# Max pooling over windows of 16: three shrinking load slots replaced by two shifted slots of 64 KB, and the last store issued from ScalarE

## Chip, cores and metric

One core of one Trainium2 chip. The metric is device time in microseconds (us). Before the change the median was 335.19 us in six runs (335.11 to 335.36). Lower is better.

## The reference

Each row of 4096 float32 numbers is cut into 256 windows of 16, and each window gives its maximum:

```python
x: (32, 256, 4096) float32
result[:, :, i] = np.max(x[:, :, start:end], axis=-1)   # 256 windows of 16
result: (32, 256, 256) float32
```

The input is 134.22 MB and the output 8.39 MB. There is one comparison per number read, so data movement is what can be expected to set the time. Spread over 128 partitions, each partition has 16,384 windows. "Column" below means one window of one partition: 64 B of input, 4 B of output.

## The kernel before

The kernel loads some columns of all partitions into a slot, lets VectorE reduce them to maxima, keeps the maxima in SBUF (the on-chip memory), and stores them all at the end. It has three slots, used in turn, in the same memory as the maxima. Because the maxima grow, the slots shrink: the loads have 128, 1024, 1024, then three each of 1000, 940, 884, 832 and 784, then 736 and 152 columns, 20 in all. All DMAs are issued from SyncE.

```python
    AREA = 53200
    SLOTS = 3
    MOST = 65536 // (4 * W)          # 1024 columns
    FIRST = 128
    ...
    area = pool.tile([P, AREA], fp32, tag="area", name="area")
    ...
        for i, size in enumerate(loads):
            a = b - size
            at = n_loads % SLOTS * slot_sizes[n_loads // SLOTS] * W
            slot = area[:, at : at + size * W]
            nc.sync.dma_start(out=slot, in_=xg[:, a * W : b * W])
            nc.vector.reduce_max(
                out=area[:, base + a : base + b],
                in_=slot.rearrange("p (n w) -> p n w", w=W),
                axis=mybir.AxisListType.X,
            )
    ...
    for dst, src in stores:          # three stores, after all loads
        nc.sync.dma_start(out=dst, in_=src)
```

Of the kernel before, what the change touches and what calls it, by code (L numbers as in the profile page):

```python
# [1 line left out]

# [4 lines left out]


@with_exitstack
def kernel(  # L10
    ctx: ExitStack,
    tc: tile.TileContext,
    x: bass.AP,
    output_size: bass.AP,
    out: bass.AP,
):





    nc = tc.nc
    P = nc.NUM_PARTITIONS
    fp32 = mybir.dt.float32

    B, C, L = x.shape
    O = int(output_size)
    assert L % O == 0, (L, O)
    W = L // O
    total = B * C * O // P  # L30
    assert B * C * O % P == 0

    AREA = 53200
    SLOTS = 3
    MOST = 65536 // (4 * W)
    ALIGN = 4
    FIRST = 128
    ROUNDS_A = 3
    LAST = 4


    slot_sizes = [MOST]
    rounds = [[FIRST] + [MOST] * (SLOTS - 1)]
    left = total - sum(rounds[0])
    while left:
        room = AREA - (total - left)
        n = min(room // (SLOTS * W + SLOTS) // ALIGN * ALIGN, MOST)
        if left <= slot_sizes[-1]:
            n = left
        slot_sizes.append(n)  # L50
        rounds.append([])
        while left and len(rounds[-1]) < SLOTS:
            n = min(n, left)
            rounds[-1].append(n)
            left -= n
    sizes = [n for r in rounds for n in r]
    groups = [sizes[: ROUNDS_A * SLOTS], sizes[ROUNDS_A * SLOTS :]]

    pool = ctx.enter_context(tc.tile_pool(name="pool", bufs=1))
    area = pool.tile([P, AREA], fp32, tag="area", name="area")  # L60

    xw = x.flatten_outer_dims().rearrange("r (o w) -> (r o) w", w=W)
    ow = out.flatten_outer_dims().rearrange("r o -> (r o)")

    stores = []
    n_loads = 0
    first = 0
    low = AREA
    for g, loads in enumerate(groups):
        n = sum(loads)  # L70
        xg = xw[first : first + P * n].rearrange("(p n) w -> p (n w)", p=P)
        og = ow[first : first + P * n].rearrange("(p n) -> p n", p=P)
        first += P * n
        base = low - n
        b = n
        for i, size in enumerate(loads):
            a = b - size
            at = n_loads % SLOTS * slot_sizes[n_loads // SLOTS] * W
            slot = area[:, at : at + size * W]
            nc.sync.dma_start(out=slot, in_=xg[:, a * W : b * W])  # L80
            nc.vector.reduce_max(  # L81
                out=area[:, base + a : base + b],
                in_=slot.rearrange("p (n w) -> p n w", w=W),
                axis=mybir.AxisListType.X,
            )
            n_loads += 1
            b = a
        low = base
        if g < len(groups) - 1:
            stores.append((og, area[:, base : base + n]))  # L90
        else:
            end = sum(loads[len(loads) - LAST :])
            for a, b in ((end, n), (0, end)):
                stores.append((og[:, a:b], area[:, base + a : base + b]))

    for dst, src in stores:
        nc.sync.dma_start(out=dst, in_=src)


# [1 line left out]
_INS = ['x', 'output_size']  # L101
_OUTS = [((32, 256, 256), 'float32')]

_NUMBERS = {'output_size': 256}


# [26 lines left out]
```

## Time and profile before

| | before |
|---|---|
| median time | 335.19 us |
| span of the profiled run | 333.4 us |
| VectorE busy | 276.0 us, 83% |
| packets of the DMA queue | 3312, 142.61 MB, 99.1% of 16 engines' span |
| loads and stores | 20 and 3 |

Lines of the page of the kernel before. "q1" is the queue that SyncE feeds; the last number of its line is the time that its packets took, as a share of 16 engines' span. In the line of VectorE (DVE) the figures are busy time and mean ns of one reduction, then the time that the engine stood idle and what ended it.

```profile
span 333.4 us, 112 instructions
DVE 276.0 (83%) x20; POOL 0.2 (0%) x4
q1 hardware_dynamic: 3312, 142.61, 99.1%
L81 DVE TENSOR_REDUCE area<-area 128x1000 f32<-128x16000 f32 (+8 forms) x20 | 276.0, 13806 | 49.1 <-DMA area<-in_x_dram 49.1
```

The DMA engines are full and VectorE waits for them and for nothing else. The timeline of the same run shows the rhythm: start, duration, then what ran, and in brackets the idle time before it.

```profile
63.17 16.82 DVE L81 TENSOR_REDUCE area<-area 128x1000 f32<-128x16000 f32 x1 [1.69 <-DMA area<-in_x_dram]
82.14 16.82 DVE L81 TENSOR_REDUCE area<-area 128x1000 f32<-128x16000 f32 x1 [2.15 <-DMA area<-in_x_dram]
...
294.93 30.58 SPq L97 DMA_DIRECT2D out_dram<-area  x3
296.14 13.22 DVE L81 TENSOR_REDUCE area<-area 128x784 f32<-128x12544 f32 x1 [1.62 <-DMA area<-in_x_dram]
310.14 15.01 DVE L81 TENSOR_REDUCE area<-area 128x736 f32<-128x11776 f32 x2 [0.77 <-DMA area<-in_x_dram]
```

A load of 1000 columns (8.19 MB) lands every 18.9 us, and its reduction takes 16.8. The last reduction ends at 325.15 us; the two large stores were issued long before and keep the DMA engines busy past that moment.

The trace also records every DMA packet, one for each row of a partition: 8 rows per DMA on each of the 16 engines, followed on each engine by a packet of 4 B (0.009 us), here called the semaphore packet. A row of 64,000 B took 2.361 us, one of 9,728 B 0.371 us.

### The profile page before, as it was taken

The page shows a single profiled execution, that of the slowest core. Times are in us where ns is not written, and L with a number is a line of the kernel's source. Part 1 is how long each engine was busy: PE and PEld are TensorE (multiplying, and loading weights), DVE is VectorE, ACT ScalarE, POOL GpSimd, SP SyncE. Part 2 cuts the span into 40 slices and gives each one's busy share as a digit, 9 for nine tenths or more (in the row PEclk, how much of TensorE's full clock was granted, in tenths as well). Part 3 has the DMA queues.
Part 4 walks back from the last instruction along what each step waited for, and adds up shares of the span by engine and source line. Part 5 has one row for each costly group of instructions (what it writes and reads, how often), then busy time and mean ns, then how long its engine had stood idle before and what let it go on. Part 6 is the DMA issues. An engine that isn't in the chain of part 4 may idle for free.

```text
span 333.4 us, 112 instructions
## 1 busy us (share of the span) xinstructions
DVE 276.0 (83%) x20; POOL 0.2 (0%) x4
## 2 busy tenths in 40 slices
DVE  2009979797988989797989797989898898989990
POOL 0000000000000000000000000000000000000000
DMA  9898989898999998999999999999999999989997
GB/s 377 377 503 377 503 369 491 369 491 369 491 397 433 462 462 375 433 462 441 434 434 434 434 434 415 409 441 473 415 409 470 397 470 397 470 380 452 414 431 310
DMA packets 3312, 142.61 MB, mean 428 GB/s; under 512 B 368, under 2 KB 368, under 8 KB 368
## 3 DMA queue, kind: packets, MB, share of 16 engines
q1 hardware_dynamic: 3312, 142.61, 99.1%
HBM read 134.22 MB, written 8.39 MB: 428 GB/s over the span
## 4 chain that ended last, share of the span: by engine, by line
DMA 64%; DVE 31%; DVEq 1%; another core or an unknown queue 0%; SPq 0%; issue 0%
DMA area<-in_x_dram 64%; DVE area L81 31%; DVEq L128 1%; SPq L80 0%; DVEq L81 0%
## 5 line engine op out<-in xcount | busy, mean ns | idle before, releaser
L81 DVE TENSOR_REDUCE area<-area 128x1000 f32<-128x16000 f32 (+8 forms) x20 | 276.0, 13806 | 49.1 <-DMA area<-in_x_dram 49.1
L114 POOL MEMSET const-bfloat16-1.0<- 128x1 bf16 x1 | 0.1, 102 | 0.0
L114 POOL MEMSET const-uint8-127<- 128x1 uint8 x1 | 0.1, 101 | 0.0
L114 POOL MEMSET const-float32-0.0<- 128x1 f32 x1 | 0.1, 99 | 0.2 <-issue 0.2
L114 POOL MEMSET const-float32-1.0<- 128x1 f32 x1 | 0.1, 98 | 0.0
## 6 DMA issues: line engine op xcount, KB each, us to landing
area<-in_x_dram SPq DMA_DIRECT2D x3, 8000.0 KB, 40.1
area<-in_x_dram SPq DMA_DIRECT2D x3, 7520.0 KB, 37.5
area<-in_x_dram SPq DMA_DIRECT2D x3, 7072.0 KB, 35.3
area<-in_x_dram SPq DMA_DIRECT2D x3, 6656.0 KB, 33.2
area<-in_x_dram SPq DMA_DIRECT2D x3, 6272.0 KB, 31.3
area<-in_x_dram SPq DMA_DIRECT2D x1, 5888.0 KB, 30.3
out_dram<-area SPq DMA_DIRECT2D x1, 3998.0 KB, 27.6
out_dram<-area SPq DMA_DIRECT2D x1, 2966.0 KB, 34.2
```

The costliest lines, as they stand in the source:

```text
L81: nc.vector.reduce_max(out=area[:, base + a : base + b], in_=slot.rearrange("p (n w) -> p n w", w=W), axis=mybir.AxisListType.X,)
L114: nc = _bacc.Bacc("TRN2", target_bir_lowering=False, num_devices=1)
L128: with _tile.TileContext(nc) as tc:
```

## The change

The intent: fewer and larger loads. Two slots replace three, so each can stay at 64 KB per partition (1024 columns) until the end, and 17 loads do the work of 20. With two slots a load has to wait until the one before last has been reduced. To shorten that wait, a slot is 152 columns longer than a load, and loads alternate between its low and its high end. The reduction is cut into 872 and 152 columns, in such an order that the next load overlaps only the piece that is reduced first. The first load has 132 columns. The last store (892 columns) is issued from ScalarE. The memory stays the same: 212,496 B per partition for 212,800.

```diff
-    SLOTS = 3
-    MOST = 65536 // (4 * W)
-    FIRST = 128
+    CHUNK = 1024
+    GAP = 152
+    FIRST = 132
+    LOADS_A, LOADS_B = 9, 6
     ...
+    ring = pool.tile([P, 2 * (CHUNK + GAP) * W], fp32, tag="ring", name="ring")
+    kept = pool.tile([P, total - last], fp32, tag="kept", name="kept")
     ...
+                low = n_loads % 2 * (CHUNK + GAP)
+                moved = n_loads // 2 % 2
+                at = low + moved * GAP
+                nc.sync.dma_start(out=ring[:, at * W : (at + n) * W], in_=xn)
+                if n == CHUNK:
+                    cut = CHUNK - GAP if moved else GAP
+                    parts = [(0, cut), (cut, n)]
+                    for u, v in parts if moved else parts[::-1]:
+                        pooled(dst[:, u:v], at + u, v - u)
     ...
+    nc.scalar.dma_start(out=og[:, full : full + last], in_=last_kept)
+    tc.no_sync_barrier()
     for dst, src in stores:
         nc.sync.dma_start(out=dst, in_=src)
```

(Cut: the slots of before, the grouping of the loads, and the last load, whose maxima lie in a free part of its slot.)

More of the change, by code (lines that the diff above doesn't have):

```diff
@@ L31 @@
     assert B * C * O % P == 0
-    AREA = 53200
-    SLOTS = 3
-    MOST = 65536 // (4 * W)
-    ALIGN = 4
-    FIRST = 128
-    ROUNDS_A = 3
-    LAST = 4
-    slot_sizes = [MOST]
-    rounds = [[FIRST] + [MOST] * (SLOTS - 1)]
-    left = total - sum(rounds[0])
-    while left:
-        room = AREA - (total - left)
-        n = min(room // (SLOTS * W + SLOTS) // ALIGN * ALIGN, MOST)
-        if left <= slot_sizes[-1]:
-            n = left
-        slot_sizes.append(n)
-        rounds.append([])
-        while left and len(rounds[-1]) < SLOTS:
-            n = min(n, left)
-            rounds[-1].append(n)
-            left -= n
@@ L56 @@
-    sizes = [n for r in rounds for n in r]
-    groups = [sizes[: ROUNDS_A * SLOTS], sizes[ROUNDS_A * SLOTS :]]
+    CHUNK = 1024
+    GAP = 152
+    FIRST = 132
+    LOADS_A, LOADS_B = 9, 6
+    last = total - FIRST - (LOADS_A + LOADS_B) * CHUNK
+    assert 0 < last and last * (W + 1) <= CHUNK * W
     pool = ctx.enter_context(tc.tile_pool(name="pool", bufs=1))
-    area = pool.tile([P, AREA], fp32, tag="area", name="area")
+    ring = pool.tile([P, 2 * (CHUNK + GAP) * W], fp32, tag="ring", name="ring")
@@ L62, with pooled, group @@
+    kept = pool.tile([P, total - last], fp32, tag="kept", name="kept")
     xw = x.flatten_outer_dims().rearrange("r (o w) -> (r o) w", w=W)
     ow = out.flatten_outer_dims().rearrange("r o -> (r o)")
+    def pooled(dst, at, n):
+        nc.vector.reduce_max(
+            out=dst,
+            in_=ring[:, at * W : (at + n) * W].rearrange("p (n w) -> p n w", w=W),
+            axis=mybir.AxisListType.X,
+        )
+    taken = 0
+    def group(n):
+        nonlocal taken
+        span = slice(taken * P, (taken + n) * P)
+        taken += n
+        return (
+            xw[span].rearrange("(p n) w -> p (n w)", p=P),
+            ow[span].rearrange("(p n) -> p n", p=P),
+        )
@@ L65 @@
     stores = []
     n_loads = 0
-    first = 0
-    low = AREA
-    for g, loads in enumerate(groups):
-        n = sum(loads)
-        xg = xw[first : first + P * n].rearrange("(p n) w -> p (n w)", p=P)
-        og = ow[first : first + P * n].rearrange("(p n) -> p n", p=P)
-        first += P * n
-        base = low - n
-        b = n
-        for i, size in enumerate(loads):
-            a = b - size
-            at = n_loads % SLOTS * slot_sizes[n_loads // SLOTS] * W
-            slot = area[:, at : at + size * W]
-            nc.sync.dma_start(out=slot, in_=xg[:, a * W : b * W])
-            nc.vector.reduce_max(
-                out=area[:, base + a : base + b],
-                in_=slot.rearrange("p (n w) -> p n w", w=W),
-                axis=mybir.AxisListType.X,
-            )
-            n_loads += 1
-            b = a
-        low = base
-        if g < len(groups) - 1:
-            stores.append((og, area[:, base : base + n]))
-        else:
-            end = sum(loads[len(loads) - LAST :])
-            for a, b in ((end, n), (0, end)):
-                stores.append((og[:, a:b], area[:, base + a : base + b]))
+    base = 0
@@ new lines @@
+    for g, loads in enumerate(
+        ([FIRST] + [CHUNK] * LOADS_A, [CHUNK] * LOADS_B + [last])
+    ):
+        xg, og = group(sum(loads))
+        a = 0
+        for n in loads:
+            xn = xg[:, a * W : (a + n) * W]
+            dst = kept[:, base + a : base + a + n] if n != last else None
+            if n == FIRST:
+                nc.sync.dma_start(
+                    out=ring[:, CHUNK * W : (CHUNK + n) * W], in_=xn
+                )
+                pooled(dst, CHUNK, n)
+            else:
+                low = n_loads % 2 * (CHUNK + GAP)
[7 more added lines that the diff above has]
+                        pooled(dst[:, u:v], at + u, v - u)
+                else:
+                    end = (at + CHUNK) * W
+                    last_kept = ring[:, end - n : end]
+                    pooled(last_kept, at, n)
+                n_loads += 1
+            a += n
+        full = a - last if g else a
+        stores.append((og[:, 0:full], kept[:, base : base + full]))
+        base += full
@@ L96 @@
+    assert taken == total
+    nc.scalar.dma_start(out=og[:, full : full + last], in_=last_kept)
+    tc.no_sync_barrier()
     for dst, src in stores:
```

## The prediction

> **What bounds the kernel now.** Data movement. The page's span is 333.4 us; the DMA queue's packets took 99.1% of 16 engines' span, 142.61 MB at a mean 428 GB/s, while VectorE was busy 276.0 us (83%) and its 49.1 us of idling waited on loads. In the trace's packet records a row of 64,000 B takes 2.361 us, one of 9,728 B 0.371 us; a fit over all rows gives 27.22 GB/s per engine (435.6 for 16) plus 0.0136 us per row. That agrees with the Trainium skill, "DMA: Bandwidth & Descriptors", section "Where 436 GB/s comes from" (435.2 GB/s through 16 ports). From the first packet, 1.76 us after the start, to the last end 330.3 us pass, of which packets fill 330.2 on each engine. So there is hardly a gap to win: outside lie 1.76 us at the start and 1.3 us at the end.
>
> **What the change does, costed.**
> - Bytes: unchanged; at the fitted rate 327.4 us.
> - Rows: 20 loads and 3 stores become 17 and 3, 8 rows per engine each: 184 rows per engine become 160. Saved: 24 x 0.0136 = 0.33 us, plus three semaphore packets of 0.009 us, all on the critical path.
> - VectorE: 15 loads are reduced in two pieces. Its durations fit 16.67 ns per output column plus 0.15 us, so 872 + 152 columns take 17.4 us for 17.22. Off the path: a load takes 19.35 us.
> - Two slots for three: load k+2 may go when the 872-column piece of load k is done, 14.7 us after k landed, and its packets flow about 1.1 us later (the first load: issued at 0.73, first packet at 1.76). The earliest engine runs out of load k+1 about 18.2 us after k landed (19.35 less 0.5 landing lag and 0.6 spread of the engines). About 2 us of slack, so no gap. Reducing in one piece would give 17.2 + 1.1 = 18.3 us, a tie; that is what the shifted slot buys.
> - End: after the last load lands (about 312.4 us) two stores of 7.93 MB occupy the engines for 18.4 us. The last store is issued from ScalarE 15.1 us after that landing, with packets at about 16.2, before the others drain at about 17.5. It interleaves with the second store; the Trainium skill, same page, section "Issuing engines are not separate DMA queues", says all issuers share the same 16 DMA engines, so this gains no bandwidth. Before, the last store was hidden too: issued at 325.2, its packets began at 328.5, directly behind the previous store.
> - Start: 132 columns for 128; the first packet does not move.
>
> **Prediction.** 335.2 - 0.35 = about 334.9 us, range 334.2 to 335.8. Chances: faster by over 2% 0.01, within 2% 0.97, slower by over 2% 0.02.
>
> **What would show each step.** DMA packets on the page fall from 3312 to 2880, their share staying near 99%; 65,536 B rows still take 2.42 us; reductions of 872 columns take 14.7 us and start every 19.35 us; VectorE totals about 278 us; the last reduction ends near 327.4 us, and the ScalarE store's packets lie among the second large store's.
>
> **What would make it wrong.** (1) Starvation: if issue to flow takes over 3 us in mid-stream, some 14 loads each leave a gap and landings are over 19.35 us apart. (2) The new row pitches (598,272 and 450,304 B for 511,744 and 536,832) slow HBM reads: rows take over 2.42 us. (3) The ScalarE store comes late and the engines idle at the end, or interleaving two queues is slower than one.

## The result, and the profile after

| | before | after |
|---|---|---|
| median of 6 runs each | 335.19 us | 335.05 us (334.90 to 335.14) |
| span of the profiled run | 333.4 us | 333.4 us |
| VectorE busy | 276.0 us | 276.5 us |
| DMA packets | 3312 | 2880 |

The ratio is 0.9995, with a 95% interval of 0.9983 to 1.0008. A ratio here is the mean time of one kernel's runs over that of the other's runs of the same rounds, so it is not quite the ratio of the medians. The time lies in the predicted range, and the difference is not clear of noise.

The same lines of the page after. "q10" is ScalarE's queue.

```profile
span 333.4 us, 113 instructions
DVE 276.5 (83%) x32; POOL 0.2 (0%) x4
q1 hardware_dynamic: 2736, 142.15, 98.7%
q10 hardware_dynamic: 144, 0.46, 0.3%
```

The reductions after, by shape:

```profile
L52 DVE TENSOR_REDUCE kept<-ring 128x872 f32<-128x13952 f32 x15 | 220.3, 14686 | 46.0 <-DMA ring<-in_x_dram 46.0
L52 DVE TENSOR_REDUCE kept<-ring 128x152 f32<-128x2432 f32 x15 | 40.1, 2676 | 0.0
```

The timeline after, in mid-stream and at the end:

```profile
102.58 17.28 DVE L52 TENSOR_REDUCE kept<-ring 128x872 f32<-128x13952 f32 x2 [2.07 <-DMA ring<-in_x_dram]
...
121.92 17.28 DVE L52 TENSOR_REDUCE kept<-ring 128x872 f32<-128x13952 f32 x2 [2.06 <-DMA ring<-in_x_dram]
...
313.27 15.01 DVE L52 TENSOR_REDUCE ring<-ring 128x892 f32<-128x14272 f32 x1
328.32 0.37 ACTq L109 DMA_DIRECT2D out_dram<-ring  x1
```

A load now lands every 19.35 us, 8.39 MB each time, which is 433.5 GB/s; before it was 8.19 MB in 18.9 us, 433 GB/s: the same rate. The DMA engines were full before and are full after. The chain of waits after shows how two slots work together (start, duration, what):

```profile
39.87 0.02 issue
39.88 23.97 DMA ring<-in_x_dram
63.86 0.02 issue
63.88 14.70 DVE kept L52
78.58 0.02 issue
78.59 23.96 DMA ring<-in_x_dram
```

One slot's cycle is 14.70 us until the first piece is reduced and 23.96 us from the issue of the next load to its landing: 38.7 us, two transfers of 19.35 us. Of the 23.96 us, the packet records give 3.6 us to waiting: load 3 (the small first load is load 0) was issued at 39.88 us and the earliest engine began it at 43.47. I call these 3.6 us the **lead**, the time for which a load is queued before the first engine has nothing else to do. The prediction had reckoned that about 1.1 us of it are needed and that the rest is slack. The experiments test that.

### The profile page after: what moved, and what is told of

Read it like the earlier page. It is cut to its first block, busy times and chain, and to the rows that moved or that the text cites. A ratio compares the mean times of both kernels' runs of the same rounds, so it can differ in the third digit from the quotient of the medians.

```text
span 333.4 us, 113 instructions
## 1 busy us (share of the span) xinstructions
DVE 276.5 (83%) x32; POOL 0.2 (0%) x4
## 2 busy tenths in 40 slices
DMA packets 2880, 142.61 MB, mean 428 GB/s; under 512 B 320, under 2 KB 320, under 8 KB 448
## 3 DMA queue, kind: packets, MB, share of 16 engines
q1 hardware_dynamic: 2736, 142.15, 98.7%
HBM read 134.22 MB, written 8.39 MB: 428 GB/s over the span
## 4 chain that ended last, share of the span: by engine, by line
DMA 58%; DVE 36%; DVEq 5%; issue 0%; SPq 0%
DMA ring<-in_x_dram 58%; DVE kept L52 36%; DVEq L143 5%; SPq L83 0%
## 5 line engine op out<-in xcount | busy, mean ns | idle before, releaser
L52 DVE TENSOR_REDUCE kept<-ring 128x872 f32<-128x13952 f32 (+2 forms) x31 | 261.5, 8477 | 51.8 <-DMA ring<-in_x_dram 51.8
L52 DVE TENSOR_REDUCE ring<-ring 128x892 f32<-128x14272 f32 x1 | 15.0, 15009 | 0.0
```

The lines of the kernel that those rows point to most:

```text
L52: nc.vector.reduce_max(out=dst, in_=ring[:, at * W : (at + n) * W].rearrange("p (n w) -> p n w", w=W), axis=mybir.AxisListType.X,)
```

## The experiments

Twelve kernels ran, all with correct results. The theory was that of the prediction: the time is bytes at a fixed rate plus a small cost per row, and everything else is off the path, with slack. The main rivals were that rows cost nothing, that the ScalarE store or the row pitch (the distance between rows in HBM) matters, and that the shifted slots do more than the prediction granted them.

### The changed kernel again, and its last store on SyncE

> The changed kernel once more, for comparison on the same chip. Theory (bytes at a fixed rate plus 0.0136 us per row): 334.8 to 335.2 us, 0.1 to 0.35 us under the kernel before. Rival (rows cost nothing, the 0.14 us seen is noise): the same median as the kernel before, on either side of it.

Measured: 334.95 us (334.83 to 335.00) beside 335.14 us for the kernel before, ratio 0.9993 (0.9981 to 1.0005). A second time the median is 0.1 to 0.2 us lower, which fits the theory; the interval still contains 1, so the rival is not excluded by time alone.

```diff
-    nc.scalar.dma_start(out=og[:, full : full + last], in_=last_kept)
-    tc.no_sync_barrier()
     for dst, src in stores:
         nc.sync.dma_start(out=dst, in_=src)
+    nc.sync.dma_start(out=og[:, full : full + last], in_=last_kept)
```

> The last store goes out on SyncE, behind the two large ones, as in the kernel before. Theory: the store is issued about 328.3 us, 2 us before the large stores drain, and follows them without a gap, so the time stays within 0.3 us of the changed kernel. Rival (the ScalarE store costs or gains something at the end, such as a second queue or its later flow): a difference of 0.5 to 1.5 us, in either direction.

Measured: 335.11 us, ratio to the kernel before 0.9999 (0.9987 to 1.0011). That is within 0.3 us of the changed kernel, as the theory had it. The packet records say why: the store's first packet starts at 330.32 us from ScalarE and at 330.33 us from SyncE, in both cases as the first engine finishes its large stores. Its issue, at 328.3 us, is early enough either way.

The mirror of it, the kernel before with its last store moved to ScalarE:

```diff
+    dst, src = stores.pop()
+    nc.scalar.dma_start(out=dst, in_=src)
+    tc.no_sync_barrier()
     for dst, src in stores:
         nc.sync.dma_start(out=dst, in_=src)
```

> The kernel before with only the last store (1228 KB) moved to ScalarE, ahead of the others. Theory: its bytes and rows are the same, so within 0.15 us of the kernel before. Rival (the changed kernel's 0.15 us come from the ScalarE store, since the version with that store on SyncE gave 335.11 for 334.95): 0.1 to 0.3 us faster than the kernel before.

Measured: 335.29 us beside 335.11, ratio 1.0005 (0.9992 to 1.0019). It did not get faster (0.18 us slower by the medians, a little more than the theory's 0.15), so the rival finds no support, though the interval reaches 0.3 us to the other side: the ScalarE store is worth nothing that these runs resolve. The Trainium skill, "DMA: Bandwidth & Descriptors", section "Issuing engines are not separate DMA queues", fits this: it says that all issuers end on the same 16 engines.

### What a row costs

```diff
-                nc.sync.dma_start(out=ring[:, at * W : (at + n) * W], in_=xn)
+                for u in range(0, n, PIECE):          # PIECE = 256
+                    v = min(u + PIECE, n)
+                    nc.sync.dma_start(
+                        out=ring[:, (at + u) * W : (at + v) * W],
+                        in_=xn[:, u * W : v * W],
+                    )
```

> Each load of 1024 columns goes out as four of 256: 45 or more extra loads, 8 rows per engine each. Theory (0.0136 us per row on each engine, 0.009 us per semaphore packet, all on the path): 48 extra loads, 384 extra rows per engine, 5.2 us + 0.4 us, so about 340.7 us (339.8 to 341.5), with rows of 16,384 B taking 0.615 us. Rival (rows cost nothing of their own while the queue is full): within 0.5 us of the changed kernel.

The page of this run has 6,912 more packets on SyncE's queue than that of the changed kernel (2736):

```profile
q1 hardware_dynamic: 9648, 142.15, 99.2%
```

Measured: 339.22 us (338.99 to 339.38), just under the theory's range and 4.27 us over the changed kernel of the same rounds (334.95). Rows do cost, so the rival falls; but 4.27 us over 384 rows per engine are 0.0111 us per row, semaphore packets included, where the theory had 5.6 us, or 0.0147 us per row. The rows themselves took 0.615 us each, as expected. What the sum of the records overlooked is that an engine's packets overlap a little: in this run they add up to 335.5 us per engine, while only 334.1 us pass from the first packet to the last end. With the cost measured here, the change's 24 fewer rows are worth 24 x 0.0111 = 0.27 us, an estimate from this run. The run does not part the cost of a row from that of a DMA, for here as in the change there are 8 rows per engine to a DMA.

### The slots without the shift

```diff
-                moved = n_loads // 2 % 2
+                moved = 0
...
-                    for u, v in parts if moved else parts[::-1]:
-                        pooled(dst[:, u:v], at + u, v - u)
+                    pooled(dst, at, n)
```

> No shifted slots and one reduction per load: a slot comes free 17.24 us after its load landed, for 14.7. Theory: a slot's cycle is 0.5 us landing lag + 19.35 us transfer + about 0.3 us spread + 17.24 us reduction + about 1.05 us from issue to flow = 38.45 us, and two transfers take 38.70 us, so it is a tie: within 0.5 us of the changed kernel, landings still 19.35 us apart. Rival (the shifted slot is what makes two slots work): landings 19.8 to 20.5 us apart and a time of 341 us or more.

Measured: 353.29 us (351.75 to 356.5), ratio 1.0542. The theory's "tie" was wrong by 18 us. The chain of waits of this run:

```profile
61.63 24.64 DMA ring<-in_x_dram
86.27 0.02 issue
86.30 17.23 DVE kept L52
103.53 0.02 issue
103.54 24.43 DMA ring<-in_x_dram
...
226.75 23.05 DMA ring<-in_x_dram
```

The reduction takes 17.23 us as expected. But issue to landing takes 22.5 to 24.6 us, 23.7 on average of loads 3 to 15, nearly the 23.96 us of the changed kernel, although there is now almost nothing left to wait behind. The sum of the expectation for it was 1.05 + 19.35 + 0.5 + 0.3 = 21.2 us. The packet records name the missing 2.5 us. Load 3, issued at 42.29 us, does start on the first engine at 43.47, 1.2 us later, but on the last one only at about 46.3 us. Its first rows took up to 3.1 us for the usual 2.42, and rows of later loads up to 3.8 us. From then on the 16 engines end each load up to 2.8 us apart, for 0.6 before. The slot comes free only when the slowest of them has landed, while the fastest one runs dry.

### Less shift: where does the loss begin?

```diff
+    SHIFT = 64                                  # then 16, then 112
...
-                at = low + moved * GAP
+                at = low + moved * SHIFT
...
-                    cut = CHUNK - GAP if moved else GAP
+                    cut = CHUNK - SHIFT if moved else SHIFT
```

> The changed kernel with its slots shifted by 64 columns for 152: a slot's part comes free 16.15 us after its load landed (960 columns), its next load's packets can flow about 1.0 us later, 17.15, and the earliest engine runs dry 18.3 us after that landing. Theory (what costs is only an engine running dry, and then a slow restart with rows of up to 3.8 us): 1.1 us in hand, so no loss, 334.8 to 335.2 us. Rival (the loss grows with every us of later release): about half of the 18.3 us that the plain slots lost, 340 us or more.

> A shift of 16 columns: free after 16.95 us, flow at about 17.95 us, 0.35 us before the earliest engine runs dry. The plain slots (17.24 us, flow at 18.25) ran dry by about 0.1 us and lost 18.3 us. Theory (a cliff at running dry): no loss, or a few of the loads restart; under 337 us. Rival (the last microsecond before running dry already costs): 345 us or more.

Measured: 345.03 us (343.26 to 347.55) and 349.38 us (348.49 to 349.93). The theory of a cliff at running dry falls: with a shift of 64 columns loads 3 and 4 were issued 2.2 us before the first engine ran dry, packets could flow after 1.0 us, and 9.9 us were lost all the same. The rival of a gradual loss holds. A third point was run to see whether the changed kernel has room to spare:

> A shift of 112 columns. The time between a load's issue and the moment the earliest engine runs dry is 3.6 us in the changed kernel (no loss), 2.2 us with a shift of 64 (9.9 us lost), 1.6 us with 16 (14.3 us lost), 1.15 us with none (18.2 us lost); with 112 it is 2.95 us. Theory C (the loss grows steadily as the lead falls below about 3.4 us, some 8 us for each us): about 4 us lost, 337.5 to 340.5 us. Rival D (a lead of somewhat over 2.2 us is enough and 152 has room to spare): no loss, 334.8 to 335.3 us.

Measured: 336.96 us (335.82 to 338.00), ratio 1.0051 (1.0020 to 1.0082). This lies between the two expectations: rival D (room to spare) falls, and theory C was too steep here. All five points together. "Lead" is from the issue of load 3 to the first engine's start on it; "lost" is the median less that of the kernel before in the same rounds; the last three columns are counted in the packet and semaphore records of the profiled run (the spread over loads 4 to 15, landing to landing from load 3 to load 15).

| shift, columns | reduced before release, us | lead, us | lost, us | rows of 64 KB over 2.5 us, of 1920 | spread of a load's 16 landings, mean us | landing to landing, us |
|---|---|---|---|---|---|---|
| 152 (changed kernel) | 14.7 | 3.6 | -0.2 | 12 | 0.59 | 19.35 |
| 112 | 15.4 | 2.9 | 1.9 | 59 | 1.31 | 19.49 |
| 64 | 16.2 | 2.2 | 9.9 | 203 | 1.66 | 19.85 |
| 16 | 17.0 | 1.6 | 14.3 | 206 | 2.17 | 20.29 |
| none | 17.2 | 1.2 | 18.2 | 283 | 2.17 | 20.32 |

The lead in the table is that of load 3, when the engines are still 0.4 to 0.7 us apart. It shrinks as they drift apart: in later loads it went down to 2.2 us with a shift of 112 and to about 1 us with 64.

The chain of waits with a shift of 64 shows the same loss as above, in small:

```profile
60.59 0.02 issue
60.61 23.34 DMA ring<-in_x_dram
83.95 0.02 issue
83.97 16.16 DVE kept L53
```

16.16 + 23.34 us make 39.5 for the 38.7 us of the changed kernel. The records don't number the engines, but a packet can be given to the engine whose last one ended just then. Ordered so, the extra time sits in the first row that an engine takes of a load: with a shift of 64, 0.3 us on average over 16 engines and up to 1.8 us for one, from load 4 on (load 3, with the same lead of 2.2 us, still came through without delay), while from the third row on the mean is 0.04 us or less. In the changed kernel the first row has no more than 0.02 us on average. The next slot comes free only with the slowest engine, so the span follows that one, and the engines ahead run dry. The packets of this profile add up to 335.9 us per engine, and 338.4 us pass from the first to the last end, where both are 330.3 us in the changed kernel: of the 8.1 us by which this execution was longer, 5.6 are slower rows and 2.5 idle engines. Without any shift it was 9.6 and 9.1 us. No run delayed the issue alone and left the slots as they are; `pitch_512k` below comes nearest, with the full shift and one late load.

### Is the needed lead a matter of the row's length?

A guess: an engine prepares the next row while it moves the current one, so a load must be queued before the last row of the load ahead begins, one row (2.42 us) plus 1.0 us before the end. That would give 3.4 us, which fits the table. With quarter rows it would be 1.6 us, and a lead of 2.2 us would do.

The edit combines the two above: SHIFT = 64 and PIECE = 256.

> The shift of 64 columns that lost 10 us, with each load sent as four of 256 columns (rows of 16,384 B, 0.615 us, for 65,536 B, 2.42 us). The load is issued 2.2 us before the earliest engine runs dry, as in that run. Theory A (the next load's first row starts without delay only if it is queued before the engine begins its last row, so the lead needed is 1.0 us from issue to flow plus one row: 3.4 us with long rows, 1.6 us with quarter rows): no loss beyond the cost of more rows, 339.0 to 340.0 us, like the quarter loads with the full shift (339.22). Rival B (the lead needed is a fixed time of about 3 us, whatever the row): most of the 10 us is lost again, 346 us or more.

Measured: 347.37 us (346.14 to 347.86), 8.2 us over the quarter loads with the full shift. Theory A falls, rival B holds: short rows do not make the short lead good. What takes the lead is not shown. The Trainium skill, same page, section "Latency and other measured facts", gives 0.6 us to the first byte for a DMA issued from SyncE or ScalarE. The very first load agrees, if the time is counted from the end of the issue: that ran from 0.73 to 1.11 us, and the first packet began at 1.74. But this is the time to a first packet; in these runs the stream needed about 3 us or more for all 16 engines to begin their part without delay.

### Stores among the loads

If stores could overlap with loads, 18 us of stores at the end would be the place to win. This run sends the first group's store as soon as its maxima are there:

```diff
         full = a - last if g else a
+        if not g:
+            nc.scalar.dma_start(out=og, in_=kept[:, base : base + full])
+            base += full
+            continue
         stores.append(...)
```

> The large store of the first group goes out from ScalarE as soon as its results are there, amid the loads, instead of after them. Theory (an engine moves one row at a time, in either direction, at 27.2 GB/s): the 4.79 MB still take 11.1 us of engine time, landings slip by 11 us in all; and at the end only 7.3 us of store are left to cover the last reduction of 15.0 us and 1 us to flow, so about 9 us stand idle: 343 to 345.5 us. Rival (stores overlap with loads, reads and writes having ways of their own): landings hardly slip, 332 to 335 us.

Measured: 345.96 us (345.71 to 346.41), a little over the theory's range. The timeline of this run:

```profile
197.04 0.38 ACTq L106 DMA_DIRECT2D out_dram<-kept  x1
199.09 17.28 DVE L52 TENSOR_REDUCE kept<-ring 128x872 f32<-128x13952 f32 x2 [2.08 <-DMA ring<-in_x_dram]
...
231.22 17.28 DVE L52 TENSOR_REDUCE kept<-ring 128x872 f32<-128x13952 f32 x2 [14.86 <-DMA ring<-in_x_dram]
...
325.94 0.35 SPq L116 DMA_DIRECT2D out_dram<-kept  x1
340.87 0.34 ACTq L113 DMA_DIRECT2D out_dram<-ring  x1
```

The load beside the store landed 32.1 us after the one before it, 12.8 us late, where the store alone is worth 11.1 us of engine time (8 rows of 1.387 us in the changed kernel). So this store did not overlap with the load, and the mixture was 1.7 us slower than one after the other (the store's rows took 1.49 us among loads, for 1.39). The rest of the loss is at the end, where one store is too short to cover the last reduction. The stores belong where both kernels have them.

### The distance between rows in HBM

> The changed kernel with a first load of 128 columns for 132; the row pitches become 598,016 and 450,560 B, which are even multiples of 256 B where the changed kernel's are odd. Theory: pitch has no effect while the rows run at 27.22 GB/s, and the slower start of the changed kernel (rows of the first load 0.54 to 0.65 us above their median per engine, for 0.35) is chance or belongs to the pitch: within 0.2 us of the changed kernel, rows of 65,536 B at 2.42 us. Rival (the 132 is there for the pitch): rows over 2.45 us, and 338 us or more.

Measured, with FIRST = 128 as the only edit: 334.74 us (334.60 to 334.90) beside 335.11, ratio 0.9988 (0.9975 to 1.0000). Rows of 65,536 B took 2.42 us, so the 132 is not there for the rate of the loads, and the rival falls. It is the lowest time of all kernels here, though by an amount that the interval hardly separates from nothing. The slow start of the first load did not go away with 128 columns (0.54 us per engine over the median row, 0.54 and 0.58 in two profiles of the changed kernel, 0.55 in the kernel before with its ScalarE store), so the 0.35 of the first profile of the kernel before was the odd one: chance, and not the change.

```diff
-    LOADS_A, LOADS_B = 9, 6
+    LOADS_A, LOADS_B = 8, 7
...
-        ([FIRST] + [CHUNK] * LOADS_A, [CHUNK] * LOADS_B + [last])
+        ([CHUNK] * LOADS_A, [FIRST] + [CHUNK] * LOADS_B + [last])
```

> The first load moved to the second group, so that each group has 8192 columns and rows lie 524,288 B apart, a power of two (598,272 and 450,304 B in the changed kernel). Theory (pitch is hidden while the 16 engines are the limit): rows of 65,536 B at 2.42 us and 335 to 336 us. Rival (a power-of-two pitch halves the rate of reads[...]): rows well over 3 us, 400 us or more.

Measured: 339.46 us (two runs). The rival falls: the median row of 65,536 B still took 2.418 us with rows exactly 512 KiB apart. The recorded rival appealed to the Trainium skill for the halved rate; that is cut above, because I had misread the page. "DMA: Bandwidth & Descriptors", section "Latency and other measured facts", gives, for copies between HBM tensors, 207 GB/s at a pitch of 512 KiB beside 214 at a padded one, so almost the full rate; the loss by half is given for 4 MiB and more, which no run here tried. The run, with loads into SBUF, agrees with the page. The 4.3 us have another place. The edit puts the small load between two groups, where it must wait for a whole slot; it was issued at 156.85 us and the first engine began it at 157.81, a lead of 1.0 us:

```profile
156.85 0.33 SPq L83 DMA_DIRECT2D ring<-in_x_dram  x1
...
183.87 17.28 DVE L52 TENSOR_REDUCE kept<-ring 128x872 f32<-128x13952 f32 x2 [5.44 <-DMA ring<-in_x_dram]
```

It landed 5.66 us after the load ahead, where its 8 rows of 0.319 us make 2.6, so 3.1 of the 4.3 us were lost at this one place, and VectorE then waited 5.44 us for the next load, for about 2.1 otherwise. After it the 16 landings of a load lie up to 2.9 us apart, as with too little shift.

Yet the loads that follow lose next to nothing: loads 11 to 15 had leads of only 1.5 to 2.3 us at the first free engine and still landed 19.34 to 19.38 us apart. For the last engine to come free they were queued 4.2 to 4.5 us ahead. This suggests that the lead at the slowest engine is what counts; no run tests it by itself. Its lowest value was 4.15 us in the changed kernel, and 3.5, 2.7, 2.0 and 1.7 us with shifts of 112, 64, 16 and none.

So this run answers the question of pitch by its rows, not by its total.

## Why the prediction was right, point by point

- **The bound: right.** Both kernels keep the 16 engines full. After the change 330.25 us pass from the first packet to the last end, before 330.31. The prediction's 435 GB/s for a full stream agrees with the Trainium skill, "DMA: Bandwidth & Descriptors", section "Where 436 GB/s comes from" (435.2 GB/s): a row's 65,536 B in 2.42 us are 27.1 GB/s on each of 16 engines, 433 GB/s.
- **Saved rows: right in kind, somewhat too large.** "24 x 0.0136 = 0.33 us" is 0.27 us at the 0.0111 us per row that the quarter loads measured. The medians moved by 0.14 and 0.19 us. Two other kernels with the same 24 fewer rows moved by 0.03 us (last store on SyncE) and 0.37 us (first load of 128 columns). So the size of the gain is not shown; only that it is small.
- **VectorE: right.** 14.69 us for 872 columns (14.7 predicted), starts 19.35 us apart. Its total is 276.5 us for 278 predicted.
- **The end and the start: right in the time.** The last reduction ended at 328.3 us for 327.4, and no gap opened. But the store's packets did not lie among those of the second large store, as predicted: the first began 2.0 us after issue, not 1.1, when all rows of the large stores had been begun. In time this changed nothing, on either engine.
- **Two slots: right in the result, wrong in the reason.** "About 2 us of slack, so no gap" and "Reducing in one piece would give 17.2 + 1.1 = 18.3 us, a tie" failed. The lead in the changed kernel is 3.6 us, and the runs show a loss of 1.9 us of time at a lead (of load 3) of 2.9 and 18.2 us at 1.2. So there is hardly any slack, and the shifted slot is worth 18 us, not the step from a tie to safety. That the changed kernel kept enough lead was luck as far as the prediction goes: its own sum gave 1.1 us as enough. The prediction took the 1.0 us from issue to the first packet as all that a load needs, and left out that the engines' first rows run late when a load is queued less than about 3 us ahead, and that the next slot then waits for the slowest engine.

Why then does a change with so many parts move the time by almost nothing? Three slots before kept most of a load in reserve (load 16, for one, was issued at 249.94 us and begun at 265.37, a lead of 15.4 us), at the price of smaller loads. Two shifted slots just keep the queue ahead of the engines, and the larger loads win back 24 rows. Both end at the same limit of bytes.

## What to carry to other kernels

When the DMA engines are full, first reckon the bytes at the measured rate; what remains is the cost of rows, here 0.011 us each, and no rearrangement of slots or issuers tried here moved the median down by more than 0.4 us. In a ring of slots, compare not whether a load is issued before the engines run dry but how long before: look in the trace for the lead, the time of each load's first rows, and the spread of its landings, and distrust a short lead until a run clears it: here 3.2 to 3.6 us in an undisturbed stream cost nothing (the changed kernel, and the loads of `pitch_512k` before its small one), and 2.9 us did. Two slots can be enough if the reduction is ordered so that the part which the next load overwrites is done first.

## What the Trainium skill lacked or had wrong

- "DMA: Bandwidth & Descriptors" gives the latency to the first byte (0.6 us, which the first load here confirms) but not how far ahead a load must be queued for a stream without loss: leads of 3.6, 2.9, 2.2, 1.6 and 1.2 us lost -0.2, 1.9, 9.9, 14.3 and 18.2 us, and rows four times shorter did not help (347.37 us). The leads are those of load 3.
- The same page's costs per packet are those of small transfers; it has none for long rows from SyncE: 0.011 us per row on each engine, semaphore packets included (4.27 us for 384 more rows, cut to 16 KB each).
- No page says whether a store among loads overlaps with them: here it did not (12.8 us later for 11.1 us of store).
